# Differential queries in one memory array per chunk and loaded ahead of the keys, pooling in single steps under merge gate tiles, four merge gate tiles moved forward

## The chip, the core and the metric

The program runs on one core of a Trainium2 chip. Times are device microseconds (us) of one execution. Three runs of the kernel before took 2752.95, 2755.56 and 2758.76 us; the profile is of a fourth execution, which took 2752.83 us.

## What is computed

Two layers work on 1024 latent tokens and 256 context tokens, each a vector of 1024 channels. In each layer (cut to what matters here):

```
h = modulated rms_norm of the tokens
z = h @ w_in                      # pool_in, mla_*, diff_q/k/v, swa_q/k/v, gates, merge
y_pool = pool_mixer(z.pool_in)    # four groups: mean over 2, 4, 8 or 16 tokens, minus the token; times w_pool
y_mla  = dense attention, 4 heads, queries and keys from a low rank
y_diff = 4 heads: softmax(q1 k1) v - lam * softmax(q2 k2) v, then rms_norm
y_swa  = windowed attention (128 tokens each way) plus the context, with a sink
m = sum over r of sigmoid(z.merge[r]) * ((y[r] * silu(z.gates[r])) @ w_br[r])
x = x + gate * rms_norm(m @ w_out)
```

The second layer has no outputs for the context tokens, so there the queries, the gates and the pooling run over 1024 tokens, not 1280.

## The kernel before

Everything lies transposed: channels on the 128 partitions, tokens along the free dimension, in chunks of 512, 512 and 256 tokens (`ALL`; in layer 1 `qch` has the two of 512 only). Every fp32 product is made of three products of a high and a low part (`mm3`, L74 to L78): `wh*xh`, `wh*xl`, `wl*xh`. A column tile of `w_in` has 128 columns; its weight is fetched (`wraw`), then split by ScalarE (`wh`) and GpSimd (`wl`, `Stream.split`). One such tile over a chunk of 512 tokens is 24 matmuls of 512 columns into one of two PSUM buffers (`pd`). The planned cost of one of its eight steps is 3 * n / 512 * 0.216 us (L315), so a tile is planned at 12.96 us over three chunks and at 10.37 us over two.

A layer runs in this order. First come the three tiles from which the low-rank queries and keys are made. Then the column tiles stand in one list, `dense.items`, filled from L786 on: differential values (2 tiles), differential keys (2), differential queries (2), gates (8), then windowed values, windowed keys, windowed queries (2), the two pooling tiles, and two tiles of merge gates (`early`, columns `W_M + 26` and `W_M + 29`). The list is worked off until the second query tile is done and the low-rank projections are finished; what is left of it is handed out in small pieces between the steps of the attentions. `dense.fill(us)` takes as many planned us from the list as it is told: 15 (layer 0) or 13 (layer 1) before the first unit of attention, then 4.75, 4.9 and 1.5 (4.5, 4.6, 1.5) over each unit of differential, latent and windowed attention (`FILL`, L1599). A unit is two blocks of 128 queries of one head (in the windowed part one block of two heads): its scores (`pss`, L1137, L1096, L1195), a softmax by VectorE (L998) and ScalarE, then turns of transposes (L1026), their split into `th` (ScalarE) and `tl` (VectorE), and products with the values (`acc`, L1042). A turn is at least two steps behind its softmax.

Some work is not in the list itself but in a queue of generators, `vals`. Its steps fall due by the planned time that the list has used: every `yield u` puts the next step u planned us later, and `vals.drain()` runs what is left at once.

The instructions are issued on each engine in an order that is fixed before the run, by a list of priorities and estimated durations, so the order on an engine can differ a little from the order in the program. DMAs are all issued by SyncE's queue (SP), in order, and wait there for what they depend on. Dependences through device memory are kept by array: a load from `dqd` waits for every write to `dqd` that is ahead of it in the program.

The places that the change touches:

- `roped` (L636) makes rotated queries and keys: the first tile of a pair leaves its half in `zt1` (one buffer), the second one's evacuation does the rotation (six VectorE and two GpSimd operations a chunk, `t1`, `t2`, and two splits) and writes to memory. For the differential queries the memory is `dqd`, one array over all 1280 tokens, written for each chunk as that chunk ends.
- `diff_units`, `load` (L1120): the query tile `qt` of a unit is read from `dqd` for 256 tokens by two DMAs. `keys` loads a head's two key tiles `kt` (four DMAs each) and the values `vt`. `prefetch` (L1217) issues keys first and then the queries of the next unit. Ahead of windowed attention it first runs the list up to the second windowed query tile, if that is not done (L1221).
- `pooled` (L724): each pooling tile's evacuation copies into `up`; after it a list item without matmul tile, `rest`, does for each chunk two (first tile) or four (second tile) additions on VectorE, yields 0.3, does a copy, a product, a difference and the split into two parts, issues the three matmuls with `w_pool` behind them, and yields 0.4.
- `merge_gate` (L717) keeps a merge gate tile's result in memory (`zmd`), from which the merge stage at the end reads it back (`reload`, L1448) in place of a weight and its 24 matmuls a chunk.

Of the kernel before, what the change touches and what calls it, by code (L numbers as in the profile page):

```python
# [32 lines left out]
def kernel(ctx: ExitStack, tc: tile.TileContext, A: dict, out: bass.AP):  # L33
# [76 lines left out]
    zmd = dram.tile([2, 128, T], F, name="zmd")  # L110
# [409 lines left out]
    def layer(l, es_prev):  # L520
# [112 lines left out]
        def heads_inner(a):  # L633
            return a.rearrange("h d n -> d h n")

        def roped(w, dst, chunks, scale, heads, hd, tabs):  # L636
            keep = {}

            def ev1(ps, c0, n):
                if c0 == 0:  # L640
                    vals.drain()
                    keep[0] = p2.tile([128, T], F, name="zt1", tag="zt1", bufs=1)
                act(keep[0][:, c0:c0 + n], ps, scale=scale)
            dense.tile(st, w, chunks, ev1)

            def ev2(ps, c0, n):
                z2 = f32("zc", n)
                act(z2, ps, scale=scale)
                z1_ = keep[0][:, c0:c0 + n]
                ct, sb = keep["t"]  # L650
                for half in range(2):
                    t1 = f32("t1", n)
                    t2 = f32("t2", n)
                    tt(t1, (z1_, z2)[half], ct, ALU.mult)
                    tt(t2, (z2, z1_)[half], sb, ALU.mult, nc.gpsimd)
                    tt(t1, t1, t2, (ALU.subtract, ALU.add)[half])
                    hs = slice(half * hd, half * hd + hd)
                    spl(t1, lambda h: dma(heads_inner(dst[0, :, hs, c0:c0 + n]), h),
                        lambda h: dma(heads_inner(dst[1, :, hs, c0:c0 + n]), h))
            def pre(c0, n):  # L660
                keep["t"] = table(tabs[0], c0, n), table(tabs[1], c0, n)
            dense.tile(st, w + 1, chunks, ev2, pre)
# [51 lines left out]
                dma(zgd[j, :, c0:c0 + n], z)  # L714
            dense.tile(st, W_G + j, qch, ev)

        def merge_gate(e, i):  # L717
# [6 lines left out]
        def pooled():  # L724
            LP = 8 + SEQ + 8 + CTX + 8
            H_, L_ = slice(64, 128), slice(0, 64)
            wph = p2.tile([128, 2, 128], R, name="wph", bufs=1)
            wpl = p2.tile([128, 2, 128], R, name="wpl", bufs=1)
            spc = p2.tile([128, 2], F, name="spc", bufs=1)
            keep = {}  # L730

            def pos(c0):
                return c0 + 8 if c0 < SEQ else c0 + 16

            def weights():
                wpr = f32("zc", 256).rearrange("p (a b) -> p a b", a=2)
                nc.gpsimd.memset(wpr, 0.0)
                for g in range(4):
                    o = 64 * (g % 2)
                    dma(wpr[o:o + 64, g // 2, o:o + 64], A["w_pool"][l, g])  # L740
                split(wpr, wph, wpl)
                dma(spc, A["s_pool"][l].rearrange("(j p) -> p j", p=128))

            for j in range(2):
                def ev(ps, c0, n, j=j):
                    if c0 == 0:
                        vals.drain()
                        if j == 0:
                            weights()
                        keep[j] = p2.tile([128, LP], F, name="up", tag="zt1", bufs=1)  # L750
                        nc.gpsimd.memset(keep[j], 0.0)
                    act(keep[j][:, pos(c0):pos(c0) + n], ps)
                dense.tile(st, W_POOL + j, qch, ev)

                def rest(j=j):
                    for c0, n in qch:
                        up = keep[j][:, pos(c0) - 8:pos(c0) + n + 8]
                        w = n + 16
                        a = f32("t1", w)
                        b = f32("t2", w)  # L760
                        tt(a[:, 1:w], up[:, 0:w - 1], up[:, 1:w], ALU.add)
                        if j == 0:
                            tt(b[H_, 8:8 + n], a[H_, 7:7 + n], a[H_, 9:9 + n], ALU.add)
                        else:
                            tt(b[:, 2:w - 1], a[:, 1:w - 2], a[:, 3:w], ALU.add)
                            tt(a[:, 4:w - 3], b[:, 2:w - 5], b[:, 6:w - 1], ALU.add)
                            tt(b[H_, 8:8 + n], a[H_, 4:4 + n], a[H_, 12:12 + n], ALU.add)
                        yield 0.3 * n / 512
                        nc.vector.tensor_copy(out=b[L_, 8:8 + n], in_=a[L_, 8:8 + n])
                        rc = f32("tab", n)  # L770
                        dma(rc, A["rcnt"][j, :, c0:c0 + n])
                        t1 = f32("tab", n)
                        tt(t1, b[:, 8:8 + n], rc, ALU.mult)
                        tt(t1, t1, up[:, 8:8 + n], ALU.subtract)
                        hl_ = {}
                        spl(t1, lambda h: hl_.__setitem__(0, h), lambda h: hl_.__setitem__(1, h))
                        ps = dense_ps(n)
                        mm3(ps, lambda k: wph[:, j], lambda k: wpl[:, j], lambda k: hl_[0], lambda k: hl_[1], [0], 1)
                        yv = f32("zc", n)
                        act(yv, ps, scale=spc[:, j:j + 1])  # L780
                        dma(yd[0][j, :, c0:c0 + n], yv)
                        yield 0.4 * n / 512
# [7 lines left out]
        roped(W_DK, dkd, ALL, 1.0, 8, 16, ("C32", "S32"))  # L790
        roped(W_DQ, dqd.rearrange("m a d n -> a m d n"), qch, 32 ** -0.5, 8, 16, ("C32", "S32"))
# [315 lines left out]
        def diff_units():  # L1107
            for h in range(4):
# [120 lines left out]
        def close_row(r):  # L1229
            s = ssum[r]  # L1230
# [39 lines left out]
        while pend:  # L1270
            dense.fill(1.0)
            pend.pop(0)()
        dense.until(early[-1])
        es_a.close()
        es_p.close()

# [148 lines left out]
        for q, (r, d) in enumerate(order):  # L1425
            i = W_M + r * 8 + d
            if q + 1 == len(order):
                st.load((l, W_O), use=0)
            elif i not in early:
                st.load((l, i + 2 if i + 1 in early else i + 1))  # L1430
            braw = tp.tile([128, 2, 128], F, name="braw", tag="braw", bufs=1)
            dma(braw, A["w_br"][l, r, d])
            bh = tp.tile([128, 2, 128], R, name="bh", tag="bh")
# [26 lines left out]
            body = reload(early.index(i)) if i in early else st.body((l, i), qch, ev)  # L1460
            some(body, KT)
            if prev:
                if prev[1] == 0:
# [251 lines left out]
```

## Time and profile before

| | |
|---|---|
| median of 3 runs | 2755.56 us |
| profiled execution, its span | 2752.83 us, 2749.9 us |
| TensorE busy | 2616.0 us (95%) |
| VectorE, ScalarE, GpSimd busy | 1526.6, 1190.7, 801.2 us |
| mean granted TensorE clock | 0.973 |
| layer 0: differential, latent, windowed attention | from 247.6, 497.2, 740.1 us |
| layer 1: the same | from 1703.0, about 1912, about 2130 us |

A share of busy time of TensorE counts a matmul to its modelled end, so that one follows on another before the first has ended; 95% is not 95% of its peak. The granted clock is 1.00 at 2.4 GHz and 0.50 at 1.2 GHz; in between it is the mean of a stretch that had both. In a timeline the bracket at the end of a row is the engine's idle time before the instruction, and what ended it.

### The profile page before, as it was taken

Reading aid. Unit: us, or ns where it says so; the run is one execution under the profiler, and the core shown is the slowest. Engines: PE = TensorE matmul, PEld = TensorE weight load, DVE = VectorE, ACT = ScalarE, POOL = GpSimd, SP = SyncE. Lnnn points to the kernel's source line nnn. Section 1 sums busy time; section 2 is a strip of 40 time slices with the busy share of each in tenths; the row PEclk is TensorE's granted clock in tenths of the full one; section 3 lists DMA queues with packets and bytes.
Section 4 is the critical chain, followed back from the end, with each engine's and each line's share of the span. In section 5 each row is a group of like instructions: output and inputs, shape, how many; then the busy total and the mean of one; then the engine's idle time right before and its main releaser. Section 6 shows DMA issues by size and latency. Waiting matters only on the chain. (4 is left out here: it accounts for less than half of the span.)

```text
span 2749.9 us, 38514 instructions
## 1 busy us (share of the span) xinstructions
PE 2616.0 (95%) x14194; PEld 2205.1 (80%) x14194; DVE 1526.6 (56%) x2638; ACT 1190.7 (43%) x2188; POOL 801.2 (29%) x492
## 2 busy tenths in 40 slices
PE   7998999999999998999999998999998999999998
PEld 5777878888888887888878776888887878888878
DVE  7544778656665686333147653888666642222333
ACT  4433666655474221222245442776554742222231
POOL 4223433111000223444323322443010013344424
PEclk9998999999999999999999998999999999999999
DMA  6376333433334553222125366433433333322223
GB/s 238 103 198 208 116 96 92 115 118 115 94 109 122 170 182 124 77 77 66 54 92 179 101 205 207 133 94 106 136 100 94 112 118 98 98 79 79 79 73 100
DMA packets 211950, 327.00 MB, mean 119 GB/s; under 512 B 27060, under 2 KB 124466, under 8 KB 211762
## 3 DMA queue, kind: packets, MB, share of 16 engines
q1 hardware_dynamic: 211762, 324.55, 38.0%
q8 instruction: 111, 1.82, 0.3%
q14 instruction: 77, 0.63, 0.1%
HBM read 241.43 MB, written 80.22 MB: 117 GB/s over the span
## 5 line engine op out<-in xcount | busy, mean ns | idle before, releaser
L76 PE MATMUL pd<-h,wh 128*128 128x512 f32 (+2 forms) x2288 | 863.1, 377 | 24.6 <-ACT sg L50 11.9
L78 PE MATMUL pd<-h,wl 128*128 128x512 f32 (+2 forms) x2288 | 847.9, 371 | 0.4 <-POOL wl L53 0.4
L77 PE MATMUL pd<-h,wh 128*128 128x512 f32 (+2 forms) x2288 | 846.1, 370 | 0.0
L53 POOL TENSOR_TENSOR wl<-wraw,wh 128x1024 fp32r<-128x1024 f32 x106 | 260.7, 2459 | 926.3 <-ACT wh L50 886.2
L76 PEld LDWEIGHTS pd<-h,wh 128*128 128x128 f32 (+1 forms) x2288 | 437.0, 191 | 87.4 <-ACT sg L50 12.9
L78 PEld LDWEIGHTS pd<-h,wl 128*128 128x128 f32 (+1 forms) x2288 | 435.4, 190 | 70.2 <-POOL wl L53 1.8
L77 PEld LDWEIGHTS pd<-h,wh 128*128 128x128 f32 (+1 forms) x2288 | 437.3, 191 | 57.8 <-DVE h L56 0.8
L998 DVE CUSTOM_DVE_ANT_0 P<-pss,zero 128x1280 f32<-128x1280 f32 (+1 forms) x216 | 295.8, 1370 | 147.0 <-PE pss L1137 75.7
L53 DVE TENSOR_TENSOR tl<-pt,th 128x512 fp32r<-128x512 f32 (+1 forms) x420 | 277.0, 671 | 149.9 <-ACT th L50 146.4
L50 ACT ACTIVATE th<-pt 128x512 fp32r<-128x512 f32 (+1 forms) x420 | 239.6, 581 | 141.8 <-PE pt L1026 136.4
L1026 PE MATMUL pt<-kc,P 128*128 128x128 f32 x1632 | 256.6, 276 | 6.1 <-POOL P L53 1.6
L53 DVE TENSOR_TENSOR sg<-sg,pt 128x512 f32<-128x512 f32 x96 | 65.7, 687 | 349.9 <-PE pt L78 349.4
L1042 PE MATMUL acc<-th,vt 128*128 128x256 f32 x816 | 240.9, 309 | 7.5 <-ACT ot L50 6.6
L1042 PE MATMUL acc<-tl,vt 128*128 128x256 f32 x816 | 219.5, 290 | 16.6 <-DVE tl L53 16.5
L50 ACT ACTIVATE wh<-wraw 128x1024 fp32r<-128x1024 f32 x124 | 130.7, 1054 | 208.7 <-PE pd L77 139.1
L50 ACT ACTIVATE P<-P,m 128x1280 f32<-128x1280 f32 (+1 forms) x144 | 182.8, 1269 | 62.5 <-DVE m L998 62.0
L1026 PEld LDWEIGHTS pt<-kc,P 128*128 128x128 f32 x1632 | 191.6, 141 | 19.1 <-DVE P L56 5.4
L50 ACT ACTIVATE sg<-pd 128x512 f32<-128x512 f32 x120 | 70.9, 591 | 277.4 <-PE pd L78 269.3
L50 ACT ACTIVATE P<-P,negm 128x1280 f32<-128x1280 f32 (+3 forms) x144 | 146.6, 1018 | 95.0 <-DVE negm L998 94.0
L1042 PEld LDWEIGHTS acc<-th,vt 128*128 128x128 f32 x816 | 156.2, 191 | 39.0 <-ACT th L50 18.2
L53 POOL TENSOR_TENSOR m<-m,sg 128x512 f32<-128x512 f32 x96 | 131.0, 1371 | 190.8 <-DVE sg L53 189.9
L1042 PEld LDWEIGHTS acc<-tl,vt 128*128 128x128 f32 x816 | 156.2, 191 | 34.5 <-DVE tl L53 25.7
(293 smaller groups left out, 3946.5 us busy)
## 6 DMA issues: line engine op xcount, KB each, us to landing
wraw<-in_w_in_dram SPq DMA_DIRECT2D x108, 512.0 KB, 3.6
wmt<-in_w_modt_dram SPq DMA_DIRECT2D x64, 256.0 KB, 3.1
wraw<-in_w_out_dram SPq DMA_DIRECT2D x32, 512.0 KB, 3.3
yd<-ot SPq DMA_DIRECT2D x108, 128.0 KB, 2.0
kt<-dkd SPq DMA_DIRECT2D x64, 160.0 KB, 3.9
qt<-dqd SPq DMA_DIRECT2D x72, 128.0 KB, 2.8
ya<-yd SPq DMA_DIRECT2D x36, 256.0 KB, 3.1
yb<-yd SPq DMA_DIRECT2D x36, 256.0 KB, 3.0
```

The lines of the kernel that those rows point to most:

```text
L50: return nc.scalar.activation(out=o, in_=i, func=func, **kw)
L53: return (e or nc.vector).tensor_tensor(out=o, in0=a, in1=b, op=op)
L76: nc.tensor.matmul(ps, wh(k), xh(k), start=k == 0, stop=False)
L77: nc.tensor.matmul(ps, wh(k), xl(k), start=False, stop=False)
L78: nc.tensor.matmul(ps, wl(k), xh(k), start=False, stop=k == n - 1)
L998: nc.vector.tensor_tensor_reduce(out=o, in0=i, in1=zero.to_broadcast([128, nk]) if mask is None else mask, scale=-1.0, scalar=1e30 if h is ...
L1026: t = nc.tensor.transpose(pt[:, 2 * j + i, :], Ps[i][:, (g + j) * 128:(g + j + 1) * 128], ident)
L1042: nc.tensor.matmul(acc, vt[:, kts[g + j], :], x[:, j, :], start=g + j == 0 and a == 0, stop=g + j == nk - 1 and a == 1)
```

## The change

The differential queries get one memory array for each chunk. `prefetch` issues the queries' load ahead of the keys'. Each pooling tile is followed at once by a merge gate tile; both pairs come right behind the eight gate tiles and ahead of the windowed tiles. The pooling's arithmetic becomes steps in `vals`, one VectorE operation a step, 0.7 planned us apart, started 1.0 after the tile's last evacuation. One copy in it moves from VectorE to ScalarE, and the load of `rcnt` is issued first. Four merge gate tiles, (branch 3: columns 2, 4, 6; branch 2: column 2), are computed ahead of the merge stage, where there were two (branch 3: columns 2 and 5).

```diff
-    dqd = dram.tile([8, 2, 32, T], R, name="dqd")
+    dqd = [dram.tile([8, 2, 32, n], R, name=f"dqd{ci}") for ci, (_, n) in enumerate(ALL)]
...
-            for j in range(2):
-                def ev(ps, c0, n, j=j):
...
-                dense.add(f"pool{j}", None, rest)
+            def ev(ps, c0, n):
+                if c0 == 0:
+                    vals.drain()
...
+                act(keep[j][:, pos(c0):pos(c0) + n], ps)
+                if (c0, n) == qch[-1]:
+                    vals.add(rest(), 1.0)
+            dense.tile(st, W_POOL + j, qch, ev)
+
+            def rest():
+                for c0, n in qch:
+                    u = 0.7 * n / 512
...
+                    rc = f32("tab", n)
+                    dma(rc, A["rcnt"][j, :, c0:c0 + n])
+                    tt(a[:, 1:w], up[:, 0:w - 1], up[:, 1:w], ALU.add)
+                    yield u
...
+                    act(b[L_, 8:8 + n], a[L_, 8:8 + n])
+                    t1 = f32("tab", n)
+                    tt(t1, b[:, 8:8 + n], rc, ALU.mult)
+                    yield u
+                    tt(t1, t1, up[:, 8:8 + n], ALU.subtract)
+                    yield u
+                    hl_ = {}
+                    spl(t1, lambda h: hl_.__setitem__(0, h), lambda h: hl_.__setitem__(1, h))
+                    yield u
+                    ps = dense_ps(n)
...
+                    yield u
...
+        early = [(3, 2), (3, 4), (3, 6), (2, 2)]
+        for j in range(2):
+            pooled(j)
+            merge_gate(j)
         values(W_SV, svd, 0)
         keys_swa()
-        roped(W_SQ, sqd, qch, 64 ** -0.5, 4, 32, ("C64", "S64"))
-        pooled()
-        early = [W_M + 26, W_M + 29]
-        for e, i in enumerate(early):
-            merge_gate(e, i)
+        roped(W_SQ, whole(sqd), qch, 64 ** -0.5, 4, 32, ("C64", "S64"))
+        for e in range(2, len(early)):
+            merge_gate(e)
...
-                        src = dqd[2 * h:2 * h + 2].rearrange("m a d n -> (a d) m n")[:, :, c0:c0 + 256]
+                        src = dqd[c0 // 512][2 * h:2 * h + 2].rearrange("m a d n -> (a d) m n")[:, :, c0 % 512:c0 % 512 + 256]
...
+                if i not in qts:
+                    qts[i] = load()
                 if key not in kvs:
                     kvs[key] = keys()
-                if i not in qts:
-                    qts[i] = load()
...
-            elif i not in early:
-                st.load((l, i + 2 if i + 1 in early else i + 1))
+            elif (r, d) not in early:
+                st.load((l, i + 2 if order[q + 1] in early else i + 1))
```

## Rows read from the trace of the kernel before

**Rows 1.** The page: busy time of each engine, share of the span, instructions.
```profile
PE 2616.0 (95%) x14194; PEld 2205.1 (80%) x14194; DVE 1526.6 (56%) x2638; ACT 1190.7 (43%) x2188; POOL 801.2 (29%) x492
```

**Rows 2.** The waits of PE: total us, times, longest us.
```profile
PE acc L1042 <- DVE tl L53: 16.5, 14, 2.4
```

**Rows 3.** Busy time by stretch, with granted clock (PEclk), DMA share, GB/s.
```profile
2340.00:2540.00 200.00, 200.00 (x877) 164.44 (x877) 53.55 (x70) 44.86 (x71) 82.46 (x49) 1.00 0.27 85
...
660.00:680.00 20.00, 17.31 (x104) 15.36 (x103) 15.87 (x26) 9.04 (x18) 2.37 (x1) 0.83 0.38 107
...
715.00:735.00 20.00, 15.18 (x75) 12.70 (x74) 16.65 (x32) 9.26 (x19) 1.44 (x1) 0.74 0.39 118
...
2060.00:2075.00 15.00, 11.03 (x59) 9.31 (x58) 12.17 (x17) 6.62 (x12) 2.36 (x1) 0.89 0.59 151
...
2105.00:2120.00 15.00, 10.83 (x44) 8.01 (x43) 14.91 (x23) 5.72 (x10) 1.15 (x1) 0.66 0.27 88
```

**Rows 4.** The first differential score of each layer, PE timeline.
```profile
247.59 1.41 PE L1137 MATMUL pss<-kt,qt 128*128 128x512 f32 x3 [6.93 <-DMA qt<-dqd]
...
1702.97 1.41 PE L1137 MATMUL pss<-kt,qt 128*128 128x512 f32 x3 [7.30 <-DMA qt<-dqd]
```

**Rows 5.** DMA issues ahead of it, SP timeline: start, us, count.
```profile
238.19 2.46 SPq L72 DMA_DIRECT2D kt<-dkd  x5
...
241.21 1.30 SPq L72 DMA_DIRECT2D qt<-dqd  x2
...
1693.06 2.19 SPq L72 DMA_DIRECT2D kt<-dkd  x4
...
1695.81 1.29 SPq L72 DMA_DIRECT2D qt<-dqd  x2
```

**Rows 6.** The page's DMA issues: count, KB each, median us to landing.
```profile
kt<-dkd SPq DMA_DIRECT2D x64, 160.0 KB, 3.9
```

**Rows 7.** Busy time around those starts, and around two shorter stalls.
```profile
245.00:260.00 15.00, 11.14 (x33) 8.10 (x34) 3.16 (x5) 3.96 (x6) 4.74 (x2) 0.62 0.64 219
1700.00:1715.00 15.00, 11.65 (x35) 8.24 (x36) 3.16 (x5) 4.05 (x5) 4.73 (x2) 0.66 0.66 223
205.00:215.00 10.00, 6.73 (x34) 6.36 (x35) 3.89 (x8) 4.04 (x8) 2.26 (x3) 0.66 0.73 234
1670.00:1680.00 10.00, 8.85 (x28) 7.08 (x29) 2.53 (x5) 3.35 (x6) 2.96 (x2) 0.68 0.71 211
```

**Rows 8.** Pooling in layer 0, VectorE timeline.
```profile
660.87 0.69 DVE L53 TENSOR_TENSOR t<-t 64x512 f32<-64x512 f32 x1
...
662.20 0.41 DVE L769 COPY t<-t 64x512 f32<-64x512 f32 x1
...
666.90 2.55 DVE L53 TENSOR_TENSOR t<-t 64x256 f32<-64x256 f32 x1
```

**Rows 9.** The same place, GpSimd timeline.
```profile
666.81 2.37 POOL L53 TENSOR_TENSOR wl<-wraw,wh 128x1024 fp32r<-128x1024 f32 x1 [31.12 <-ACT wh L50]
```

**Rows 10.** Pooling in layer 0, PE timeline.
```profile
670.41 0.58 PE L1042 MATMUL acc<-tl,vt 128*128 128x256 f32 x1 [1.85 <-DVE tl L53]
...
719.99 0.39 PE L1096 MATMUL pss<-kt,qt 96*128 96x256 f32 x1 [0.52 <-DVE negm L998]
...
722.00 0.80 PE L76 MATMUL pd<-sh,wph 128*128 128x512 f32 x1 [1.39 <-ACT sh L50]
```

**Rows 11.** Busy time: quiet latent attention, rotated windowed queries, end of windowed attention.
```profile
575.00:600.00 25.00, 25.00 (x170) 22.83 (x169) 12.00 (x20) 12.89 (x24) 2.38 (x1) 1.00 0.16 49
605.00:640.00 35.00, 30.53 (x177) 26.34 (x176) 25.72 (x38) 17.52 (x31) 8.33 (x8) 0.95 0.51 159
...
815.00:840.00 25.00, 19.62 (x119) 16.84 (x118) 14.59 (x36) 20.12 (x45) 1.74 (x1) 0.86 0.34 107
```

**Rows 12.** Last evacuation of the differential query tiles, ACT timeline, both layers.
```profile
231.64 0.37 ACT L50 ACTIVATE zc<-pd 128x256 f32<-128x256 f32 x1
...
1690.95 0.58 ACT L50 ACTIVATE zc<-pd 128x512 f32<-128x512 f32 x1
```

More of the change, by code (lines that the diff above doesn't have):

```diff
@@ L109 @@
     zgd = dram.tile([8, 128, T], F, name="zgd")
-    zmd = dram.tile([2, 128, T], F, name="zmd")
+    zmd = dram.tile([4, 128, T], F, name="zmd")
     mq = dram.tile([2, 4, 96, T], R, name="mq")
@@ L634, in heads_inner, with whole @@
             return a.rearrange("h d n -> d h n")
+        def whole(t):
+            return lambda a, hs, c0, n: t[a, :, hs, c0:c0 + n]
         def roped(w, dst, chunks, scale, heads, hd, tabs):
@@ L657, in ev2 @@
                     hs = slice(half * hd, half * hd + hd)
-                    spl(t1, lambda h: dma(heads_inner(dst[0, :, hs, c0:c0 + n]), h),
-                        lambda h: dma(heads_inner(dst[1, :, hs, c0:c0 + n]), h))
+                    spl(t1, *(lambda h, a=a: dma(heads_inner(dst(a, hs, c0, n)), h) for a in range(2)))
             def pre(c0, n):
@@ L715, in gates, with merge_gate @@
             dense.tile(st, W_G + j, qch, ev)
-        def merge_gate(e, i):
+        def merge_gate(e):
+            i = W_M + 8 * early[e][0] + early[e][1]
             def ev(ps, c0, n):
@@ L722, in merge_gate, with pooled @@
             dense.tile(st, i, qch, ev)
-        def pooled():
+        pw = {}
+        def pooled(j):
             LP = 8 + SEQ + 8 + CTX + 8
             H_, L_ = slice(64, 128), slice(0, 64)
-            wph = p2.tile([128, 2, 128], R, name="wph", bufs=1)
-            wpl = p2.tile([128, 2, 128], R, name="wpl", bufs=1)
-            spc = p2.tile([128, 2], F, name="spc", bufs=1)
+            if j == 0:
+                pw.update(h=p2.tile([128, 2, 128], R, name="wph", bufs=1), l=p2.tile([128, 2, 128], R, name="wpl", bufs=1),
+                          s=p2.tile([128, 2], F, name="spc", bufs=1))
             keep = {}
@@ L740, in weights @@
                     dma(wpr[o:o + 64, g // 2, o:o + 64], A["w_pool"][l, g])
-                split(wpr, wph, wpl)
-                dma(spc, A["s_pool"][l].rearrange("(j p) -> p j", p=128))
-            for j in range(2):
-                def ev(ps, c0, n, j=j):
[L746 to L782, printed above, removed]
-                dense.add(f"pool{j}", None, rest)
@@ new lines, in weights @@
+                split(wpr, pw["h"], pw["l"])
+                dma(pw["s"], A["s_pool"][l].rearrange("(j p) -> p j", p=128))
+            def ev(ps, c0, n):
+                if c0 == 0:
+                    vals.drain()
+                    if j == 0:
+                        weights()
+                    keep[j] = p2.tile([128, LP], F, name="up", tag="zt1", bufs=1)
+                    nc.gpsimd.memset(keep[j], 0.0)
+                act(keep[j][:, pos(c0):pos(c0) + n], ps)
+                if (c0, n) == qch[-1]:
+                    vals.add(rest(), 1.0)
@@ new lines, in pooled @@
+            dense.tile(st, W_POOL + j, qch, ev)
+            def rest():
+                for c0, n in qch:
+                    u = 0.7 * n / 512
+                    up = keep[j][:, pos(c0) - 8:pos(c0) + n + 8]
+                    w = n + 16
+                    a = f32("t1", w)
+                    b = f32("t2", w)
+                    rc = f32("tab", n)
+                    dma(rc, A["rcnt"][j, :, c0:c0 + n])
+                    tt(a[:, 1:w], up[:, 0:w - 1], up[:, 1:w], ALU.add)
+                    yield u
+                    if j == 0:
+                        tt(b[H_, 8:8 + n], a[H_, 7:7 + n], a[H_, 9:9 + n], ALU.add)
+                        yield u
+                    else:
+                        tt(b[:, 2:w - 1], a[:, 1:w - 2], a[:, 3:w], ALU.add)
+                        yield u
+                        tt(a[:, 4:w - 3], b[:, 2:w - 5], b[:, 6:w - 1], ALU.add)
+                        yield u
+                        tt(b[H_, 8:8 + n], a[H_, 4:4 + n], a[H_, 12:12 + n], ALU.add)
+                        yield u
+                    act(b[L_, 8:8 + n], a[L_, 8:8 + n])
+                    t1 = f32("tab", n)
+                    tt(t1, b[:, 8:8 + n], rc, ALU.mult)
+                    yield u
+                    tt(t1, t1, up[:, 8:8 + n], ALU.subtract)
+                    yield u
+                    hl_ = {}
+                    spl(t1, lambda h: hl_.__setitem__(0, h), lambda h: hl_.__setitem__(1, h))
+                    yield u
+                    ps = dense_ps(n)
+                    wh_, wl_ = pw["h"], pw["l"]
+                    mm3(ps, lambda k: wh_[:, j], lambda k: wl_[:, j], lambda k: hl_[0], lambda k: hl_[1], [0], 1)
+                    yv = f32("zc", n)
+                    act(yv, ps, scale=pw["s"][:, j:j + 1])
+                    dma(yd[0][j, :, c0:c0 + n], yv)
+                    yield u
@@ L789, in layer @@
         values(W_DV + 1, dvd, 2)
-        roped(W_DK, dkd, ALL, 1.0, 8, 16, ("C32", "S32"))
-        roped(W_DQ, dqd.rearrange("m a d n -> a m d n"), qch, 32 ** -0.5, 8, 16, ("C32", "S32"))
+        roped(W_DK, whole(dkd), ALL, 1.0, 8, 16, ("C32", "S32"))
+        roped(W_DQ, lambda a, hs, c0, n: dqd[c0 // 512][:, a, hs], qch, 32 ** -0.5, 8, 16, ("C32", "S32"))
         for j in range(8):
             gates(j)
+        early = [(3, 2), (3, 4), (3, 6), (2, 2)]
+        for j in range(2):
+            pooled(j)
+            merge_gate(j)
         values(W_SV, svd, 0)
         keys_swa()
-        roped(W_SQ, sqd, qch, 64 ** -0.5, 4, 32, ("C64", "S64"))
-        pooled()
-        early = [W_M + 26, W_M + 29]
-        for e, i in enumerate(early):
-            merge_gate(e, i)
+        roped(W_SQ, whole(sqd), qch, 64 ** -0.5, 4, 32, ("C64", "S64"))
+        for e in range(2, len(early)):
+            merge_gate(e)
         p1b = pool(f"mlb{l}", 1, es_m)
@@ L1272, in layer @@
             pend.pop(0)()
-        dense.until(early[-1])
+        dense.until(W_M + 8 * early[-1][0] + early[-1][1])
         es_a.close()
@@ L1459, in layer @@
                 prep.add(gated_y(r, 1), 0.0)
-            body = reload(early.index(i)) if i in early else st.body((l, i), qch, ev)
+            body = reload(early.index((r, d))) if (r, d) in early else st.body((l, i), qch, ev)
             some(body, KT)
```

## The prediction, made before the changed kernel was run

> **What bounds the kernel now.** I read the busy times first, then the waits of TensorE, then stretches of 10 to 25 us, then single rows. TensorE is busy for 95% of the span and every other engine for 56% or less [rows 1], so time can only come from matmuls that go away or from places where TensorE waits or runs at half clock. No matmul goes away here: two merge gate tiles a layer change place, nothing is dropped. So I look for holes. The merge stage has none worth speaking of: 200.00 of 200 us busy at clock 1.00 [rows 3]. The holes are in attention. The largest entry of the waits is TensorE waiting for `tl`, 16.5 us in 14 waits [rows 2]: VectorE is late with the low halves. And there are two single stalls of 6.93 and 7.30 us at the first differential score of each layer [rows 4]. Behind each hole comes a second cost: the clock falls to its lower level (0.50, 1.2 GHz) and the next matmuls take twice as long. The stretch of 15 us behind the first of those stalls has a mean clock of 0.62, that of the second 0.66 [rows 7].
>
> **Part 1: queries by chunk, ahead of keys.** Before, `qt` waited for the last write to `dqd`, and its two DMAs were issued behind the key tiles (at 241.21 and 1695.81), in 1.30 us [rows 5]. After the change the first unit needs only the first chunk, which is written ahead of the others, and `qt` goes ahead of `kt`. What is late next is the last key tile, which the first score also needs. Its issue ended at 238.19 + 2.46 = 240.65 and at 1693.06 + 2.19 = 1695.25 [rows 5], and a key DMA lands 3.9 us after issue in the median [rows 6]: 244.55 and 1699.15. If the queries' two DMAs stand right ahead of them, both move 1.3 us back, to 245.85 and 1700.45; if they fall into an earlier gap of SP's queue, they don't. I take the later ones. Against 247.59 and 1702.97 that is 1.7 and 2.5 us of idle time saved. The clock: behind the present stalls busy time times (1 - clock) is 11.14 * 0.38 = 4.2 us and 11.65 * 0.34 = 4.0 us; behind two stalls of 4.6 and 5.0 us, about what I expect to remain, it is 6.73 * 0.34 = 2.3 and 8.85 * 0.32 = 2.8 us [rows 7]. Saved: 1.9 + 1.2. Sum of the part: 7.3 us. Ends: nothing is left of either stall, 14.2 + 8.2 = 22.4 us; or the keys were as late as the queries all along and now land 1.3 us later in each layer, a loss of 2.6.
>
> [...]
>
> **Part 2: pooling in single steps.** Four stretches hold the pooling. TensorE idles there for 2.69, 4.82, 3.97 and 4.17 us, 15.65 in all, and busy time times (1 - clock) adds 2.9 + 3.9 + 1.2 + 3.7 = 11.7 us: 27.4 us [rows 3]. VectorE is the reason: 79 to 99% busy there, 48% in a quiet stretch of the same latent attention [rows 3, 11]. Its bursts of five to nine operations of 0.69 us stand ahead of `tl` and of the softmax, and the product with `w_pool` is issued right behind its own split (1.39 us at 722.00) [rows 8, 10]. After the change one operation of 0.69 us falls due every 0.7 planned us. A latent unit is planned at 4.9 us and takes (740.1 - 497.2) / 20 = 12.1 us by the table, so a step comes every 1.7 us: 0.69 / 1.7 = 40% on top of 48%, busy but without bursts. The product has a step of 1.7 us between it and its split, against 1.3 us that a split on two engines takes when neither is held up. The copies, 0.41 us on VectorE, go to ScalarE, which is idle for about half of that stretch.
>
> What stays is the weight split on GpSimd. At 666.81 it took 2.37 us, and a pooling addition that began at 666.90 beside it took 2.55 instead of 0.69 us; then `tl` was late and TensorE idled 1.85 us [rows 8 to 10]. A tile's pooling still lasts as long as a merge gate tile, so the next tile's split still falls into it, once for each of four. I let four such stalls of 1.85 us remain, 7.4 us, with a third more for the clock, as around the rotated windowed queries (4.47 us idle, 30.53 * 0.05 = 1.5 us of clock) [rows 11]: 9.9 us. Saved: 27.4 - 9.9 = 17.5 us. Ends: 27.4, and 0 if the jam only moves; below nothing is excluded, since VectorE's work falls.
>
> The Trainium skill ("GPSIMD Engine Reference", section "1. Specifications") says that GpSimd shares its SBUF interfaces with VectorE and contends with VectorE instructions that have two SBUF inputs. All pooling additions have two, `tl` has only one. By that rule single steps don't help the held one, only the ones behind it; the trace agrees, with 2.55 us against 0.69, and this is the last of the rivals below.
>
> **Part 3: the new order of the list.** When the last latent unit of layer 0 starts (719.99), the second pooling tile's products run (722.00) [rows 10]: 14 tiles are used up, 181.4 planned us, and about 3 of pooling. In the new order 16 tiles, 207.4 us, lie up to the end of the windowed queries. So the prefetch of the first windowed unit runs some 22 planned us of tiles in one piece; in layer 1, by the same count, some 17. In itself that is TensorE at work and costs nothing, and the rotation's bursts disturb no softmax there: of the 6.0 us that the rotated queries cost now [rows 11] I count half, 3 us, as saved. But the first windowed score then waits for the rotation, the write and the load. The differential queries show that chain: from their last evacuation to the first score 247.59 - 231.64 = 16.0 us, in layer 1 1702.97 - 1690.95 = 12.0 us [rows 4, 12]. Beside it lies the rest of a latent unit, about 11 us in layer 0 and 12 in layer 1. I take a stall of 5 us in layer 0 and none in layer 1; with half again for the clock as in rows 7, 7.4 us lost. Ends: 0, and (if nothing covers) 28.0 us of stall with 8.2 of clock, 36.2.
>
> The windowed attention itself gains nothing: it loses 5.4 us and 19.62 * 0.14 = 2.7 us of clock at its end in layer 0, where the list is empty [rows 11], but the forced piece takes the two new tiles' worth, so as little is left for it as before. Moving two tiles out of a full merge stage into a full forced piece is worth zero, and four reads in place of two lie beside the dense tile that follows each.
>
> **Sum.** 7.3 + 17.5 + 3 - 7.4 = 20.4 us off 2752.83 us, 2732.4. The median of the runs shown lies 2.7 us above the profiled execution, so 2735 us.
>
> **The rivals.**
> - Slower: the start of windowed attention becomes the new wait, as `dqd` was: its cover is used up ahead of the forced piece, and the full chain of 16.0 and 12.0 us stands open with the clock behind it. 7.3 + 17.5 + 3 - 36.2 = -8.4, so 2764 us. It decides once stalls and clock there exceed 27.8 us. For it: the same chain shows openly now at `dqd` [rows 4]. Against: there the list had only 15 planned us to give, here a unit's turns lie between. 8%.
> - The stalls vanish: queries and keys are there before the list's piece ends, no split meets a pooling step, nothing waits at the windowed start: 22.4 + 27.4 + 3 = 52.8, 2703 us. A part of it, some 35 us or more, 15%.
> - The first score doesn't start earlier, since the keys land when the queries did, and windowed attention stalls as taken: -2.6 + 17.5 + 3 - 7.4 = 10.5, 2745 us. 12%.
> - The splits hold the steps as they hold the bursts, so that only the waits of the products go (4 us of the 27.4): 7.3 + 4 + 3 - 7.4 = 6.9, 2749 us. 13%.
>
> **How the numbers follow.** The forecast, 2724 to 2744, has 52%. What a measurement of this kernel can't tell from no change is 0.2%, 5.5 us: 2750 to 2761. Half of the last rival and a quarter of the one before it fall there, with some of the slow one's weaker forms: 12% for no change. Slower 8%, faster 80%. The range for 8 in 10 runs from 2709, most of the way to the vanishing stalls, to 2756, beyond the third and fourth rival.
>
> **What would show it.** The waits of TensorE for `qt` gone or under a microsecond, and in their place one for `kt` of some 5 us in each layer. `tl` waits halved, and VectorE nowhere above 90% for 15 us of latent attention. A stretch of some 20 us of `pd` matmuls alone at the end of latent attention, then a short wait of a windowed score for `qt<-sqd`. The prediction is wrong if that wait is over 10 us, if new `tl` waits appear in latent attention where the pooling now lies, or if the merge stage shows idle time at the tiles read back.

## The result, and the profile after

The changed kernel took 2717.8 us (median of 4 runs, 2714.37 to 2719.84) against 2754.26 us of the kernel before (median of 4): ratio 0.9874, 95% interval [0.9857, 0.9891], 34.7 us faster. The forecast was 2735 us with a range down to 2709, so sign and range held, though the result lies below the 2724 to 2744 us given 52%. The reason given for most of it did not hold.

The profiled execution took 2719.84 us, with a span of 2717.8 us against 2749.9, 32 us less. TensorE's line on the page, which answers to [rows 1], and the waits, which answer to [rows 2] (total us, times, longest us):

```profile
PE 2601.5 (96%) x14194; PEld 2201.4 (81%) x14194; DVE 1527.6 (56%) x2628; ACT 1200.5 (44%) x2208; POOL 804.7 (30%) x492
```

```profile
PE acc L1059 <- DVE tl L53: 16.8, 9, 4.2
...
PE pss L1154 <- DMA kt<-dkd: 9.7, 2, 5.0
...
PE pss L1154 <- DVE m L1015: 8.1, 5, 1.8
```

The `tl` waits total as much as before, in 9 waits in place of 14. The `qt` waits are gone, with `kt` waits in their place, and there are new score waits for VectorE's `m` (1.8 us in all before), the extreme of each row of scores that the exponential subtracts.

Busy time by stretch (columns as in [rows 3]: the stretch, its length, the busy time of TensorE's matmuls, of its weight loads, of VectorE, ScalarE and GpSimd, then clock, DMA share and GB/s), in the order pooling in layers 0 and 1, forced piece, windowed start in both layers, first scores in both layers:

```profile
540.00:560.00 20.00, 20.00 (x137) 18.36 (x136) 8.41 (x14) 10.44 (x18) 2.38 (x1) 1.00 0.43 118
...
580.00:600.00 20.00, 19.00 (x130) 17.14 (x128) 17.96 (x27) 11.83 (x24) 2.38 (x1) 1.00 0.13 39
1950.00:1970.00 20.00, 19.95 (x124) 17.41 (x122) 13.32 (x19) 11.09 (x20) 2.70 (x1) 1.00 0.23 73
...
714.00:738.00 24.00, 24.00 (x131) 20.83 (x130) 9.26 (x12) 5.57 (x11) 8.47 (x5) 1.00 0.33 101
738.00:755.00 17.00, 12.67 (x67) 10.89 (x66) 11.82 (x19) 7.08 (x15) 4.12 (x3) 0.80 0.58 181
2103.00:2120.00 17.00, 12.78 (x66) 11.14 (x65) 10.71 (x13) 5.49 (x10) 5.45 (x3) 0.80 0.58 192
...
246.00:261.00 15.00, 9.21 (x23) 6.75 (x24) 4.88 (x9) 6.64 (x9) 6.10 (x3) 0.54 0.85 268
1678.00:1693.00 15.00, 9.63 (x28) 7.06 (x29) 3.60 (x6) 5.03 (x6) 7.07 (x4) 0.66 0.79 254
```

Read the third number (the stretch counted as the first), TensorE, with the clock (third from the right). Pooling now lies where both are full or nearly so; before they were 17.31 of 20 at 0.83 and 15.18 of 20 at 0.74 [rows 3].

To see where 32 us went I took each stage's elapsed time and subtracted its matmuls at the pace that their starts show at full clock (0.2267, 0.1738 and 0.1172 us for 512, 384 and 256 columns; 0.12 was taken for 128 columns, whose starts are 0.109 apart in the median, and 0.11 for narrower ones; all kernels have the same matmuls, so differences between columns don't hang on it). What is left is idle time and half clock together, in us, both layers added; a stage runs from its first score (or merge product) to that of the next:

| | before | after | bursts | two tiles | own item, bursts | own item, steps | six tiles |
|---|---|---|---|---|---|---|---|
| differential | 38.9 | 46.6 | 44.3 | 44.4 | 51.4 | 51.3 | 45.4 |
| latent | 51.2 | 21.4 | 22.4 | 21.2 | 38.6 | 38.3 | 22.0 |
| windowed | 19.1 | 17.2 | 16.4 | 42.9 | 16.6 | 16.2 | 4.7 |
| merge | 31.4 | 24.8 | 25.2 | 25.1 | 27.0 | 25.2 | 22.4 |
| starts, output, end | 128.0 | 126.7 | 120.5 | 124.5 | 125.9 | 127.6 | 124.1 |
| span | 2749.9 | 2717.8 | 2710.0 | 2739.1 | 2740.7 | 2739.9 | 2699.8 |

Latent attention gave 29.8 us, differential attention took 7.7, and the merge stage gave 6.6. More than half of the 7.7 is part 1: without it (second run below) the differential stages have 42.2 us, and part 1 alone raises them from 38.9 to 44.6. The columns to the right are experiments, below. One profiled span differs from another of the same kernel by some us (the four runs shown lie within 5.5), so the verdicts go by the ratios and the table by its large steps.

One correction to the text ahead of the prediction: in `FILL`, 4.75 and 4.5 stand for a latent unit and 4.9 and 4.6 for a differential one, not the other way round. The prediction's "planned at 4.9 us" should be 4.75, and nothing of its sum hangs on that.

### The profile page after: what moved, and what is told of

It is laid out like the page before. It is cut to its first block, busy times and chain, and to the rows that moved or that the text cites. A ratio compares the mean times of both kernels' runs of the same rounds, so it can differ in the third digit from the quotient of the medians.

```text
span 2717.8 us, 38566 instructions
## 1 busy us (share of the span) xinstructions
PE 2601.5 (96%) x14194; PEld 2201.4 (81%) x14194; DVE 1527.6 (56%) x2628; ACT 1200.5 (44%) x2208; POOL 804.7 (30%) x492
## 5 line engine op out<-in xcount | busy, mean ns | idle before, releaser
L1059 PE MATMUL acc<-tl,vt 128*128 128x256 f32 x816 | 218.4, 289 | 16.9 <-DVE tl L53 16.8
## 6 DMA issues: line engine op xcount, KB each, us to landing
yd<-ot SPq DMA_DIRECT2D x108, 128.0 KB, 1.8
qt<-dqd SPq DMA_DIRECT2D x72, 128.0 KB, 3.0
```

Source lines behind the costliest of these rows:

```text
L1059: nc.tensor.matmul(acc, vt[:, kts[g + j], :], x[:, j, :], start=g + j == 0 and a == 0, stop=g + j == nk - 1 and a == 1)
```

## The experiments

Each ratio is to runs of the kernel before on the same chip, with its 95% interval.

**Is part 1 worth 7.3 us?** First alone, put into the kernel before:

```diff
-                if key not in kvs:
-                    kvs[key] = keys()
                 if i not in qts:
                     qts[i] = load()
+                if key not in kvs:
+                    kvs[key] = keys()
```

with `dqd` by chunk as in the change.

> The kernel before with the per-chunk query arrays and the queries loaded ahead of the keys, and nothing else of the change. Theory formed on the trace after: the keys' landing takes the place of the queries' (4.69 and 4.97 us of wait), the next gate tile's weights are issued as late as before or later, so the first three scores run with no dense work between them, and what the first wait gives is paid back by the next two: within 3 us of the kernel before, 2751 to 2757 us, with a wait for the mask's product of about 1.6 us at each of the second and third scores of each layer. Rival, the prediction's part 1: 7.3 us faster, about 2747 us, and no new waits.

Measured: 2750.84 us, ratio 1.0003 [0.9991, 1.0014]: between 2.5 us faster and 3.9 slower. 7.3 us are excluded. The waits came as the theory said: its first scores waited 5.21 and 5.55 us for `kt` and the next two 1.59 us each. Then the same edit taken out of the changed kernel:

> The changed kernel with the differential queries in one array and the keys loaded first, as before; pooling steps, order and four merge tiles stay. Theory: part 1 is worth about nothing, so within 4 us of the changed kernel (2714 to 2722 us), the wait of about 7 us for the queries back at each layer's first score and the waits of the next two scores gone. Rival, the prediction: 7.3 us slower than the changed kernel, about 2725 us.

Measured: 2716.47 us, ratio 0.9884 [0.9864, 0.9904], against 0.9874 [0.9857, 0.9891] with it: no difference. The start of layer 0, PE timeline, in the changed kernel

```profile
248.60 1.43 PE L1154 MATMUL pss<-kt,qt 128*128 128x512 f32 x3 [4.69 <-DMA kt<-dkd]
251.63 1.44 PE L1154 MATMUL pss<-kt,qt 128*128 128x512 f32 x3 [1.59 <-DVE m L1015]
254.65 1.22 PE L1154 MATMUL pss<-kt,qt 128*128 128x512 f32 x2 [1.59 <-DVE m L1015]
255.67 0.63 PE L76 MATMUL pd<-h,wh 128*128 128x512 f32 x1
```

and without part 1

```profile
249.29 1.40 PE L1154 MATMUL pss<-kt,qt 128*128 128x512 f32 x3 [6.86 <-DMA qt<-dqd]
251.59 0.79 PE L76 MATMUL pd<-h,wh 128*128 128x512 f32 x1 [0.90 <-ACT wh L50]
252.18 0.63 PE L77 MATMUL pd<-h,wh 128*128 128x512 f32 x1
252.61 1.05 PE L1154 MATMUL pss<-kt,qt 128*128 128x512 f32 x2
```

show why. With part 1 the first wait is 2.2 us shorter, but the first dense matmul starts 11.8 us behind the end of the last one ahead of the stall, against 9.2 us without part 1, and three scores run alone with TensorE waiting between them. The expectation calls `m` the mask's product; no mask is in it. SP's issues in the changed kernel (start, us):

```profile
238.87 0.62 SPq L72 DMA_DIRECT2D qt<-dqd  x1
...
240.88 0.56 SPq L72 DMA_DIRECT2D dqd<-sl  x1
241.49 0.62 SPq L72 DMA_DIRECT2D qt<-dqd  x1
242.16 2.90 SPq L72 DMA_DIRECT2D kt<-dkd  x6
...
245.57 0.43 SPq L72 DMA_DIRECT2D wraw<-in_w_in_dram  x1
...
247.00 0.60 SPq L72 DMA_DIRECT2D wraw<-in_w_in_dram  x1
```

The second query load is issued only behind the last write to `dqd`, and the keys follow it. That moves the keys by little: their issue ends 3.6 us behind the end of that write (241.44 to 245.06), against 2.5 us in the kernel before and in the one without part 1. The next tile's weight is issued no later, counted in the same way (4.1 us against 4.4), but in the run with part 1 alone it landed 7.9 us after its issue, against 6.2 us in the kernel before. ScalarE's split of it then stands behind the first exponential. ScalarE's timeline in the changed kernel

```profile
251.61 1.36 ACT L50 ACTIVATE P<-P,m 128x1280 f32<-128x1280 f32 x1 [9.87 <-DVE m L1015]
...
253.28 0.38 ACT L50 ACTIVATE zc<-pd 128x256 f32<-128x256 f32 x1 [0.22 <-DMA zgd<-zc]
253.56 1.05 ACT L50 ACTIVATE wh<-wraw 128x1024 fp32r<-128x1024 f32 x1
```

and without part 1

```profile
250.48 1.06 ACT L50 ACTIVATE wh<-wraw 128x1024 fp32r<-128x1024 f32 x1 [10.23 <-DMA wraw<-in_w_in_dram]
...
252.26 1.36 ACT L50 ACTIVATE P<-P,m 128x1280 f32<-128x1280 f32 x1 [0.45 <-DVE m L1015]
```

Why the weight takes longer to land was not tried.

**What gave 30 us in latent attention?** The prediction said the single steps. Here they are taken away: in the changed kernel the pooling of a chunk is two pieces again, beside the same merge gate tile; every other `yield u` of it goes as well.

```diff
                         tt(b[H_, 8:8 + n], a[H_, 4:4 + n], a[H_, 12:12 + n], ALU.add)
-                        yield u
+                    yield 0.3 * n / 512
                     act(b[L_, 8:8 + n], a[L_, 8:8 + n])
...
                     dma(yd[0][j, :, c0:c0 + n], yv)
-                    yield u
+                    yield 0.4 * n / 512
```

> The changed kernel with the pooling chunk again in two pieces (additions in one burst; copy, product, difference, split and matmul in the second), in its new place in the list and with its copy on ScalarE. Theory: the 29.8 us that the latent stages gave come from the steps between which the planner puts attention work; the bursts bring back the waits for the weight split and for the pooling product, 15 to 28 us slower than the changed kernel, 2733 to 2746 us. Rival: the gain comes from the new place in the list and from the matmul-only piece ahead of windowed attention, so the bursts cost under 5 us: 2716 to 2723 us.

Measured: 2719.01 us, ratio 0.9883 [0.9866, 0.99]. My theory failed: the steps are worth nothing that can be measured. In its profile, busy time by stretch,

```profile
580.00:600.00 20.00, 18.37 (x120) 15.87 (x119) 19.57 (x34) 12.58 (x25) 2.40 (x1) 1.00 0.31 94
```

VectorE (19.57 of 20 us) is as full as in the fullest stretch of the kernel before (14.91 of 15, at a clock of 0.66 [rows 3]), and still the clock stays at 1.00. A burst on VectorE is not enough to make a hole. The number of early tiles came next:

```diff
-        early = [(3, 2), (3, 4), (3, 6), (2, 2)]
+        early = [(3, 2), (3, 5)]
...
-        dense.until(W_M + 8 * early[-1][0] + early[-1][1])
+        dense.until(W_SQ + 1)
```

> The changed kernel with two merge gate tiles moved into attention instead of four: both are used up in latent attention, none is left behind the windowed queries, and the merge stage computes two tiles more. Theory: windowed attention loses the dense work between its score groups, which then wait for the exponentials, and the merge stage gets the same matmuls: 6 to 20 us slower than the changed kernel, 2724 to 2738 us. Rival: tiles can be computed as well in the merge stage, so the number is worth nothing: 2716 to 2721 us.

Measured: 2746.05 us, ratio 0.9985 [0.9975, 0.9995], about 30 us slower than the changed kernel, more than the theory gave. Latent attention keeps its gain (21.2 us in the table), and windowed attention loses it again (42.9 in place of 17.2). Of `pd`, the dense tiles' matmuls and the few of pooling, its windowed part has none (busy time by stretch, that tile only, without GpSimd's column):

```profile
755.00:785.00 30.00, 0.00 (x0) 0.00 (x0) 0.00 (x0) 0.00 (x0) 0.94 0.43 134
785.00:815.00 30.00, 0.00 (x0) 0.00 (x0) 0.00 (x0) 0.00 (x0) 0.89 0.31 80
```

So I looked at `pd` where the holes had been. In the kernel before, the same view of stretches of [rows 3],

```profile
660.00:680.00 20.00, 5.26 (x25) 3.45 (x24) 0.00 (x0) 1.06 (x2) 0.83 0.38 107
715.00:735.00 20.00, 6.41 (x18) 3.77 (x19) 0.00 (x0) 1.85 (x3) 0.74 0.39 118
```

and after

```profile
540.00:560.00 20.00, 11.23 (x51) 7.55 (x51) 0.00 (x0) 2.14 (x4) 1.00 0.43 118
560.00:580.00 20.00, 9.74 (x33) 5.50 (x33) 0.00 (x0) 0.60 (x1) 1.00 0.30 91
580.00:600.00 20.00, 10.11 (x45) 6.58 (x45) 0.00 (x0) 0.97 (x2) 1.00 0.13 39
```

there is about half as much of it before. Little `pd` alone makes no hole, however. The run with the bursts has a stretch of 20 us with next to none, all instructions and then `pd`:

```profile
1893.00:1913.00 20.00, 19.31 (x121) 16.61 (x120) 15.71 (x27) 15.13 (x26) 1.19 (x1) 1.00 0.38 115
```

```profile
1893.00:1913.00 20.00, 2.73 (x9) 1.24 (x7) 0.00 (x0) 1.83 (x3) 1.00 0.38 115
```

VectorE has 15.71 of 20 us there, and TensorE stays at 19.31; in the stretch of the same run above, VectorE had 19.57 and `pd` 11.95. So a hole takes both, a full VectorE and no dense matmuls at hand. Before, pooling was an item of the list, and while it was worked off no dense tile was: by TensorE's timeline the dense tiles pause at its four places for 19.5, 20.5, 16.8 and 17.2 us. Now it runs in `vals` beside a merge gate tile. That gave a new theory, cover, and its test: the run with the bursts, with the pooling an item of its own again.

```diff
-                if (c0, n) == qch[-1]:
-                    vals.add(rest(), 1.0)
             dense.tile(st, W_POOL + j, qch, ev)
...
+            dense.add(f"pool{j}", None, rest)
```

> The kernel with pooling in two pieces (the run before: 2719 us), in which the pooling is moreover a list item of its own again, worked off between its tile and the merge gate tile, and not beside that tile; the order of the tiles and the four merge gate tiles stay. Theory, formed on the run with the bursts: what the latent stages gained is cover. As an item of its own the pooling uses up turns of the list without giving TensorE a matmul of a dense tile; beside a merge gate tile it doesn't. So the holes come back: stretches of latent attention without pd matmuls, 15 to 28 us slower, 2734 to 2747 us. Rival: the place in the list alone did it (pooling no longer meets the weight splits of the last tiles), then under 5 us: 2716 to 2724 us.

Measured: 2743.87 us, ratio 0.9963 [0.9951, 0.9975], some 22 us slower than with the cover (0.9883). Order, tiles and place are the same. (The first pooling item begins at 495 us, ahead of latent attention, so a part of the loss stands in the table's differential row.) The holes are back, TensorE and VectorE (third and fifth number) and the clock in two stretches of pooling,

```profile
600.00:612.00 12.00, 9.97 (x55) 8.89 (x55) 11.38 (x21) 6.67 (x14) 0.00 (x0) 0.86 0.50 146
1986.00:2004.00 18.00, 12.05 (x51) 9.53 (x50) 13.25 (x19) 8.03 (x14) 0.78 (x1) 0.81 0.39 132
```

of which `pd` has

```profile
600.00:612.00 12.00, 2.54 (x6) 1.44 (x6) 0.00 (x0) 1.37 (x2) 0.86 0.50 146
1986.00:2004.00 18.00, 6.77 (x22) 4.63 (x23) 0.00 (x0) 1.38 (x2) 0.81 0.39 132
```

The fourth corner is single steps without cover, the same edit in the changed kernel:

> The changed kernel with the pooling in single steps, 0.7 planned us each, but as a list item of its own, not beside a merge gate tile. Theory (cover): single steps are worth nothing by themselves, and as an item they use up more planned time without a dense matmul than two pieces do (24.5 planned us in layer 0 against 3.5), so the holes are longer and shallower: at least as slow as the two pieces as an item (0.9963 of the kernel before), 2740 to 2765 us. Rival, the prediction's part 2: the steps remove the bursts on VectorE wherever they run, 15 to 20 us faster than the two pieces as an item, 2722 to 2730 us.

Measured: 2742.14 us, ratio 0.9968 [0.9956, 0.9979]. With cover, steps or bursts: 0.9874 and 0.9883. Without, 0.9968 and 0.9963. Cover is worth 0.8 to 0.9%, steps nothing. The planned time without a dense tile is not what sets the price: it is 24.5 us against 3.5 in layer 0, at the same loss. The dense tiles' real pauses are 18 to 34 us with two pieces and 27 to 45 us with steps.

**Is a tile worth what it covers?** In the changed kernel the list runs out in windowed attention: from 815 to 845 us TensorE is busy for

```profile
815.00:845.00 30.00, 27.55 (x186) 24.76 (x186) 21.42 (x47) 25.53 (x58) 2.39 (x1) 0.92 0.37 105
845.00:870.00 25.00, 24.34 (x131) 20.78 (x130) 13.36 (x25) 14.14 (x29) 2.49 (x1) 0.96 0.44 133
```

Two more tiles, `(2, 4)` and `(2, 6)` added to `early`:

> The changed kernel with six merge gate tiles in attention (branch 2, columns 4 and 6 in addition). Theory: a merge gate tile is worth what it covers; the list runs out about 55 us before the merge stage (windowed attention then keeps TensorE at 36 to 92%), and two more tiles fill a part of that: 5 to 15 us faster than the changed kernel, 2703 to 2713 us. Rival: the four tiles already cover what can be covered, and the two more are worked off in one piece behind windowed attention: within 4 us, 2714 to 2722 us.

Measured: 2702.51 us, ratio 0.981 [0.9796, 0.9825]: some 18 us below the changed kernel by the ratios, a little more than the theory gave, and the fastest ratio of all. The same stretches are full:

```profile
815.00:845.00 30.00, 30.00 (x217) 27.83 (x216) 21.39 (x47) 23.39 (x58) 2.40 (x1) 1.00 0.28 80
845.00:870.00 25.00, 24.93 (x144) 21.69 (x143) 10.63 (x23) 13.51 (x28) 2.40 (x1) 1.00 0.56 171
```

Eight tiles, `(1, 2)` and `(1, 4)` in addition, ask whether this goes on:

> The changed kernel with eight merge gate tiles in attention. Theory: a tile is worth what it covers; with six tiles TensorE is already 94 to 101% full in the last 25 us of windowed attention and ends it with matmuls alone, so two more only lengthen that piece: within 3 us of six tiles, 2698 to 2705 us. Rival: every tile moved out of the merge stage gives about 8 us, as the fifth and sixth did: 2684 to 2690 us.

Measured: 2701.16 us, ratio 0.9826 [0.981, 0.9842]. It doesn't: there is nothing left to cover, and the rival's 8 us a tile are excluded.

**Can the starts be mended?** Part 1 taken out of the kernel with six tiles:

> Six merge gate tiles, and the differential queries in one array behind the keys as before. Theory: both results so far stay as they are, six tiles about 16 us faster than four and part 1 worth nothing: within 4 us of six tiles with part 1 (0.981 of the kernel before), 2696 to 2704 us. Rival: part 1 helps once the rest is covered, then 5 us or more slower than that.

Measured: 2701.02 us, ratio 0.9823 [0.9809, 0.9838]; the interval overlaps that with part 1. Worth nothing there either. Next, the weight ahead of `qt` and `kt`:

```diff
+        dense.step()
         prefetch(0)
...
-    FILL = ({ ... "pre": 15.0},
-            { ... "pre": 13.0})
+    FILL = ({ ... "pre": 20.0},
+            { ... "pre": 18.0})
```

> The changed kernel with one step of the list taken ahead of the first prefetch, so that the next gate tile's weight is fetched ahead of qt, kt and vt, and with 20 and 18 planned us of tiles (15 and 13 before) ahead of the first unit. Theory: the first scores then have dense work beside and between them, the waits for kt (4.69 and 4.97 us), the two waits for the mask's product and the half clock behind them go: 8 to 16 us faster than the changed kernel, 2702 to 2710 us. Rival: the keys come later by as much as the weight's transfer takes, and the start only shifts: within 4 us, 2714 to 2722 us.

Measured: 2726.2 us, ratio 0.9901 [0.9888, 0.9914], some 7 us slower than the changed kernel: both theory and rival failed. The `kt` waits went down to one of 1.1 us, and starts, output and end lost 6.0 us of their idle and half clock (120.7 by the table's count). But differential attention rose to 51.2 and latent attention to 27.4. The run changes two things, the order at the start and how far the list is on when attention begins, so which of them costs it stays open.

**The forced piece ahead of windowed attention.** More dense work for each unit, so that the windowed queries end earlier:

```diff
-    FILL = ({1: 4.75, 2: 4.9, 3: 1.5, ... },
-            {1: 4.5, 2: 4.6, 3: 1.5, ... })
+    FILL = ({1: 4.75, 2: 6.1, 3: 1.5, ... },
+            {1: 4.5, 2: 5.75, 3: 1.5, ... })
```

> The changed kernel with 6.1 and 5.75 planned us of tiles over each latent unit in place of 4.9 and 4.6, so that the windowed queries are done inside latent attention and no piece of matmuls alone is forced ahead of the windowed part. Theory: the tl stall behind the forced piece (3.80 and 4.22 us, and the clock of 0.80 around it) goes, but the windowed part has less left: 0 to 8 us faster, 2710 to 2718 us. Rival: TensorE was full during the forced piece, so nothing is won and the end of windowed attention runs out of tiles earlier: 2 to 8 us slower, 2720 to 2726 us.

Measured: 2754.02 us, ratio 1.0005 [0.9995, 1.0014]: the change's whole gain lost. The edit was not the one expected: number 2 is the differential unit. So it doesn't test the forced piece. What it shows is the price of giving a unit more than it hides: its differential stages have 81.9 us of idle and half clock (46.6 in the changed kernel), and its waits

```profile
PE pss L1154 <- DVE m L1015: 24.8, 15, 3.6
PE pss L1154 <- issue: 14.9, 8, 3.1
```

are scores that come late. The edit that was meant, on the kernel with six tiles (number 1 to 5.9 and 5.6, number 3 from 1.5 to 2.0):

> Six merge gate tiles, with 5.9 and 5.6 planned us of tiles over each latent unit in place of 4.75 and 4.5, and 2.0 in place of 1.5 over each windowed unit, so that the windowed queries end inside latent attention. Theory: the tl stall behind the forced piece goes, with the half clock around it, and with six tiles the windowed part still has enough: 3 to 10 us faster than six tiles alone, 2690 to 2698 us. Rival, after the run that raised the differential numbers: more tiles over a unit than its waits hold only push the softmax behind, and new score waits cost more than the stall: 5 to 25 us slower, 2705 to 2725 us.

Measured: 2704.11 us, ratio 0.9831 [0.9817, 0.9845], against 0.981 [0.9796, 0.9825] of six tiles: about 6 us slower by the ratios, with intervals that meet. So there is no gain: the theory failed, and the lower end of the rival (5 us slower) is about what came. TensorE's longest `tl` wait fell from 4.2 to 2.1 us, but a wait of 3.69 us for `th` stands 10 us ahead of the windowed start.

## Why the prediction was right, and where it was wrong

**Where to look was right, but for the merge stage.** No matmul went away; 24.0 us of the table's 32 came from idle and half clock of TensorE in attention, most of it from the four pooling stretches. Of the signs named, `qt` waits gone, `kt` waits of 5 us and a full piece of `pd` came; `tl` waits were not halved.

**Part 1, 7.3 us expected, nothing found.** The first wait came nearly as taken. The keys' issue moved by 1.1 us where the forecast had 1.3, and the waits fell from 6.93 and 7.30 to 5.21 and 5.55 us in the run with part 1 alone and to 4.69 and 4.97 in the changed kernel: 1.7 to 2.3 us a layer, against 1.7 and 2.5 forecast. The step that failed is the one behind that wait, "behind two stalls of 4.6 and 5.0 us, about what I expect to remain, it is 6.73 * 0.34 = 2.3 and 8.85 * 0.32 = 2.8 us". Those two stalls end at a dense tile that goes on at once; TensorE's timeline before:

```profile
208.27 0.58 PE L76 MATMUL pd<-h,wh 128*128 128x256 f32 x1 [4.57 <-ACT zt L50]
...
1671.15 0.80 PE L76 MATMUL pd<-h,wh 128*128 128x512 f32 x1 [4.98 <-ACT zt L50]
```

At the first scores the dense tile isn't ready. Four waits of 1.59 us came in, 6.4 us in all, where there had been 0.90, 0.38 and 0.30. The clock was hardly saved either: 0.54 and 0.66 in the stretches of first scores, against 0.62 and 0.66 [rows 7], or 4.2 and 3.3 us by the forecast's own rule against 4.2 and 4.0. What the first wait gave, the next two and the clock took back. The part's lower end, a loss of 2.6 us, lies inside what was measured, the 7.3 us outside.

**Part 2, 17.5 us expected of the steps, nothing found.** The place was right: latent attention gave 29.8 us, a little more than the part's upper end of 27.4. The step that failed is "VectorE is the reason", with single steps as the cure. A full VectorE was half of the reason: it was as full with the bursts under cover, at clock 1.00. The other half was made by the list: for the length of a pooling item there was no dense tile to work off, and TensorE had only the attention's products, which wait for VectorE and ScalarE. The row that would have told, beside VectorE's, is `pd` in the stretches of [rows 3], 5.26 and 6.41 of 20 us; I read there which engine was busy, not which work of TensorE was missing. The diff says it as well: `dense.add("pool...", None, rest)` became `vals.add`.

The residual of 9.9 us for the weight splits was too large. Two collisions are left, both in layer 0's pooling; VectorE and GpSimd timelines after, of the second:

```profile
596.10 2.74 DVE L53 TENSOR_TENSOR tab<-t,tab 128x512 f32<-128x512 f32 x1
```

```profile
595.90 2.38 POOL L53 TENSOR_TENSOR wl<-wraw,wh 128x1024 fp32r<-128x1024 f32 x1 [37.11 <-ACT wh L50]
```

2.74 us in place of 0.69, as in [rows 8, 9]; the first took 2.56 us, at 499.12. The `tl` waits behind them are 1.41 and 1.70 us, where four of 1.85 with a third more were taken. The Trainium skill ("GPSIMD Engine Reference", section "1. Specifications") names contention of GpSimd with VectorE instructions that have two SBUF inputs, and both rows agree with it.

**Part 3.** "Moving two tiles out of a full merge stage into a full forced piece is worth zero" is the second large error. Two tiles are worth 30 us (0.9985 against 0.9874): the pooling now uses up two as its cover, and without the other two windowed attention has none. The forced piece came about as counted (22 planned us), 24.00 of 24 us busy before the windowed start in layer 0. The stall behind it was put at 5 us and none; it is 3.80 and 4.22 us, with 2.5 and 2.6 us of clock by the two rows of 17 us: 13.1 in place of 7.4. It is not the expected wait for the queries' load but `tl` behind the rotation. It lies ahead of the first windowed score, so it is a part of the 21.4 us that latent attention has left.

**Not foreseen:** the 6.6 us of the merge stage, nearly all in layer 0. The prediction's "none worth speaking of" was read in a stretch of layer 1; layer 0's merge stage had 26.1 us of idle and half clock before and 19.6 after, of which TensorE's waits for ScalarE's `sg` were 11.9 and 8.8 us. All kernels of the table with the new order have them (22.4 to 27.0), part 1 alone has them hardly (29.7), but neither has the run with 6.1 planned us (29.6), which has the new order. What does it was not tried.

So that 34.7 us came within the range around 20.4 is luck in good part, by errors that went opposite ways: two parts worth 24.8 in the forecast gave nothing, and one costed at zero, four tiles with the pooling under two of them, gave more than all of it.

## What to carry to other kernels

Beside asking which engine is late in a hole, count the work that the bottleneck engine has ready there: here a busy helper engine hurt only where nothing independent was left to issue. Side work that carries no matmuls belongs beside a tile, not between tiles, and independent tiles are worth what they cover; six here, and no more from eight. A wait that is made shorter gives nothing if the work behind it isn't ready: when a load is put first, look at what feeds the next dense work too.

## What the runs showed of the hardware

VectorE at 98% (19.57 of 20 us) left TensorE at 18.37 of 20 and the clock at 1.00, with 11.95 us of `pd` matmuls between. With 2.54 us of them in 12, and VectorE at 11.38 of 12, TensorE had 9.97 of 12 and the clock 0.86. With 2.73 us of them in 20 but VectorE at 15.71, TensorE had 19.31 and the clock 1.00. Stretches of 15 to 17 us around stalls of 3.8 to 5.0 us had a mean clock of 0.54 to 0.80: 0.80 twice where matmuls followed at once, 0.54 and 0.66 where two more waits of 1.59 us came first. A product of VectorE with two SBUF inputs of 128x512 took 2.56 and 2.74 us beside a GpSimd subtraction of 2.40 and 2.38 us, and 0.69 us alone.
